# Products of 64 rows issued as side-by-side pairs in a three-block transformer kernel, the causal mask moved to VectorE, and GDN row sums padded to 128 rows

## The chip, the cores and the metric

The kernel runs on one core of a Trainium2 chip. The core has TensorE (matmul; the profile calls it PE, and its weight loads PEld), VectorE (DVE), ScalarE (ACT), GpSimd (POOL) and a queue engine (SP) that issues DMAs. Each engine works through its own list of instructions in the order in which the program has them, and waits for the others by semaphores. The metric is the device time of one execution in microseconds, the median of several; lower is better. About 0.2% of this kernel's time (6 us) is what a measurement can tell from no change.

## What is computed

Three blocks follow each other on 512 tokens of 1024 features: a block with a state-space scan (SSD) and a gated delta rule (GDN), a block with an RWKV scan and a sparse attention (DSA), and a block with a gated MLP and a differential attention. All arithmetic is float32. The parts that the change touches, cut to their core:

```
# GDN, per chunk of tokens: row sums of log decays, spread over all partitions
decay = exp(where(tril, gc[..., :, None] - gc[..., None, :], -inf))

# DSA, block 2: 8 heads of 64 features; index scores choose the keys, then softmax
sc        = einsum('bqhd,bsd->bqhs', iq, ik) * 64 ** -0.5
idx_score = einsum('bqhs,bqh->bqs', relu(sc), iw)          # top 256 keys are kept
p = softmax(einsum('bqhd,bqkhd->bqhk', q, k_sel) * 64 ** -0.5)
out = einsum('bqhk,bqkhd->bqhd', p, v_sel)

# RWKV, block 2: 8 heads of 64 features, one step per token (the kernel does it by chunks)
state = state * w_t + (state @ -kk_t) b_t^T + v_t k_t^T ;  y_t = state @ r_t

# differential attention, block 3: 8 heads, two 64-feature queries and keys each
p1 = softmax(causal(q1 @ k1.T / 8)) ; p2 = softmax(causal(q2 @ k2.T / 8))
o  = rms_norm((p1 - lam * p2) @ v)
```

## The kernel before

Features or tokens lie on the 128 partitions, 512 tokens or 128 features along the free dimension. Nearly all matmul work is linear layers: `mm3` (L216 to L218) and `lin_tm` (L245 to L247) split every float32 operand into two float32r parts and sum three products into a PSUM bank. Their weights come in by DMA, ScalarE makes the high part (L194) and VectorE the low part (L195).

PSUM has eight banks of 512 float32 columns. `ps_lin` gives two banks with the tag "pl" to the linear layers. `ps` gives two banks each with the tags "pa", "paa" and "pab": the plain stream and the streams "a" and "b", between which heads or chunks alternate. A name like `pa_20958` in a row is one such bank while it is in use.

The instructions are recorded in program order by the functions below; a scheduler then puts them in the fixed order in which each engine runs them. It fills TensorE's list between the steps of a scan or of an attention with products of linear layers that come before or after in the program, so the rows of an attention stand mixed with rows of L216 to L218.

A product "of 64 rows" contracts over 64 features and so occupies one half of the array's rows: features 0 to 63 of a tile or 64 to 127. A plain float32 product is two instructions in the trace. These are the 64-row products:

- `attend` of block 3 (L1736 and on; twice, once per half of the heads): for each of four blocks b of 128 queries, four heads and two maps m, the scores of 128 queries against (b + 1) * 128 keys. Keys ahead of the diagonal block are one product (L1751, absent for b = 0). In the diagonal block a bfloat16 product first puts the causal mask into PSUM (L1752), and the scores are summed onto it (L1753). VectorE takes the row maximum (L1754), ScalarE the exponential from PSUM (L1756); ScalarE and VectorE merge the two maps (L1760, L1761); TensorE transposes (L1764), ScalarE copies the transposes out (L1766), TensorE multiplies with v (L1769), ScalarE copies the result out (L1770). A norm of the whole block of queries follows.
- `attend` of block 2 (L1473 and on): for each b and each of eight heads, scores (L1480), mask and maximum in one VectorE instruction (L1483), exponential (L1486), transposes (L1489), copy (L1491), product with v (L1493). The streams "a" and "b" alternate by head; one bank of the plain stream collects the result of all eight heads.
- `rwkv_scan` (L1304): per chunk 16 products of 128 columns, four at a time for one row half, then four for the other, each four into one bank.
- `prepare` of the RWKV part (L1219, L1224) and `score` of the index scores (L1136).
- The GDN row sums (L712, L834) have 64 rows as well, because two parts of 32 columns are stacked.

`select` (L1152, L1153) picks the keys by 48 rounds of maximum and replacement on VectorE; it stands in VectorE's list next to the first half of the RWKV work.

## Time and profile before

| | |
|---|---|
| median of 3 runs | 3030.83 us (3030.61 to 3033.38) |
| the profiled execution: first to last instruction | 3028.6 us |
| PE busy | 2947.4 us, 97% |
| PEld busy | 2430.1 us, 80% |
| DVE busy | 1735.4 us, 57% |
| ACT busy | 1112.4 us, 37% |
| POOL busy | 46.9 us, 2% |
| mean granted clock of TensorE | 0.989 of full speed |

The profiled execution's span is 2.2 us under the median of the timed runs. A busy share is the union of an engine's instructions over the span. The end of a matmul is modelled and matmuls overlap, so start times say more about what a matmul costs than their durations do.

### The profile page before, as it was taken

What the parts mean: (1) busy time and instruction counts of PE and PEld (TensorE: products, weight loads), DVE (VectorE), ACT (ScalarE), POOL (GpSimd) and SP (SyncE); (2) the same over time, 40 slices, a digit from 0 to 9 for tenths busy, and PEclk for the clock granted to TensorE, in tenths of its full rate; (3) what the DMA queues carried; (4) which work ended last, traced back from release to release, by engine and by line L of the source; (5) the groups of instructions that cost most, each with busy time, mean ns of one, the idle gap of its engine ahead of it and who ended that gap; (6) DMA issues with size and microseconds to landing.
All of it is one profiled execution on the core that took longest, in us unless ns stands there. A gap on an engine that the chain in (4) does not pass through costs nothing. (4 is left out here: it accounts for less than half of the span.)

```text
span 3028.6 us, 39369 instructions
## 1 busy us (share of the span) xinstructions
PE 2947.4 (97%) x15170; PEld 2430.1 (80%) x15170; DVE 1735.4 (57%) x3871; ACT 1112.4 (37%) x2076; POOL 46.9 (2%) x95
## 2 busy tenths in 40 slices
PE   6999999999999999999999999999999999999999
PEld 4778888888788886788978878888987978888887
DVE  6787737655655457977653564333757563553343
ACT  4435424433322233333253332222465553332221
POOL 1000000000000000000000000000000000000000
PEclk9999999999999998999999999999999999999999
DMA  5222233233445322222113423333321214333332
GB/s 125 78 58 77 60 96 98 68 97 98 139 144 162 91 84 85 71 59 58 34 32 87 131 83 92 98 97 102 118 70 57 63 44 131 98 91 96 99 91 90
DMA packets 481660, 269.06 MB, mean 89 GB/s; under 512 B 30607, under 2 KB 469073, under 8 KB 481473
## 3 DMA queue, kind: packets, MB, share of 16 engines
q1 hardware_dynamic: 445680, 255.67, 28.9%
q10 hardware_dynamic: 33920, 9.44, 1.3%
q0 software_dynamic: 1872, 1.43, 0.6%
q8 instruction: 120, 1.97, 0.3%
q14 instruction: 68, 0.55, 0.1%
HBM read 252.20 MB, written 14.16 MB: 88 GB/s over the span
## 5 line engine op out<-in xcount | busy, mean ns | idle before, releaser
L194 ACT CAST wh<-wr 128x1024 fp32r<-128x1024 f32 (+3 forms) x447 | 454.0, 1016 | 1293.0 <-PE pl L217 914.3
L216 PE MATMUL pl<-h,wh 128*128 128x512 f32 x2224 | 878.8, 395 | 10.0 <-DVE long L1186 4.6
L218 PE MATMUL pl<-h,wl 128*128 128x512 f32 x2224 | 875.7, 394 | 11.5 <-DVE wl L195 11.5
L217 PE MATMUL pl<-h,wh 128*128 128x512 f32 x2224 | 878.0, 395 | 1.0 <-DVE h L195 1.0
L195 DVE TENSOR_TENSOR wl<-wr,wh 128x1024 fp32r<-128x1024 f32 (+3 forms) x447 | 525.9, 1177 | 413.3 <-ACT wh L194 402.0
L216 PEld LDWEIGHTS pl<-h,wh 128*128 128x128 f32 x2224 | 419.8, 189 | 100.6 <-DVE long L1186 5.4
L218 PEld LDWEIGHTS pl<-h,wl 128*128 128x128 f32 x2224 | 419.2, 189 | 100.9 <-DVE wl L195 14.8
L217 PEld LDWEIGHTS pl<-h,wh 128*128 128x128 f32 x2224 | 419.5, 189 | 90.3 <-issue 3.5
L217 PE MATMUL pl<-long,wh 128*128 128x512 f32 x648 | 252.9, 390 | 0.2 <-DVE long L195 0.2
L216 PE MATMUL pl<-long,wh 128*128 128x512 f32 x648 | 253.1, 391 | 0.0
L218 PE MATMUL pl<-long,wl 128*128 128x512 f32 x648 | 253.0, 390 | 0.0
L543 DVE SCALAR_TENSOR_TENSOR long<-pl,long 128x512 f32<-128x512 f32 x72 | 49.8, 691 | 178.3 <-PE pl L218 178.3
L216 PEld LDWEIGHTS pl<-long,wh 128*128 128x128 f32 x648 | 121.7, 188 | 26.3 <-issue 1.0
L218 PEld LDWEIGHTS pl<-long,wl 128*128 128x128 f32 x648 | 121.7, 188 | 25.6 <-issue 0.3
L217 PEld LDWEIGHTS pl<-long,wh 128*128 128x128 f32 x648 | 121.7, 188 | 25.4 <-DVE long L195 0.7
L531 DVE TENSOR_TENSOR tmp<-tmp,pl 128x512 f32<-128x512 f32 x66 | 45.3, 686 | 149.2 <-PE pl L218 149.2
L216 PE MATMUL pl<-tmpa,wh 128*128 128x512 f32 (+1 forms) x304 | 120.1, 397 | 3.4 <-ACT tmpa L322 3.4
L217 PE MATMUL pl<-tmpb,wh 128*128 128x512 f32 (+1 forms) x304 | 120.9, 398 | 0.1
L218 PE MATMUL pl<-tmpa,wl 128*128 128x512 f32 (+1 forms) x304 | 120.2, 396 | 0.0
L216 PEld LDWEIGHTS pl<-tmpa,wh 128*128 128x128 f32 (+1 forms) x304 | 57.3, 189 | 16.8 <-ACT tmpa L322 4.0
L217 PEld LDWEIGHTS pl<-tmpb,wh 128*128 128x128 f32 (+1 forms) x304 | 57.4, 189 | 13.2 <-DVE tmpb L323 1.3
L218 PEld LDWEIGHTS pl<-tmpa,wl 128*128 128x128 f32 (+1 forms) x304 | 57.5, 189 | 13.0 <-issue 0.7
(772 smaller groups left out, 4034.5 us busy)
## 6 DMA issues: line engine op xcount, KB each, us to landing
wr<-in_w_in SPq DMA_DIRECT2D x169, 512.0 KB, 3.7
wr<-in_w_ffn_in SPq DMA_DIRECT2D x44, 512.0 KB, 4.0
wr<-in_ffn_w_gate SPq DMA_DIRECT2D x44, 512.0 KB
wr<-in_ffn_w_up SPq DMA_DIRECT2D x44, 512.0 KB, 3.8
wr<-in_ffn_w_down SPq DMA_DIRECT2D x32, 448.0 KB, 3.7
wr<-in_w_ada SPq DMA_DIRECT2D x24, 512.0 KB, 3.5
wr<-in_w_out SPq DMA_DIRECT2D x16, 512.0 KB, 3.9
wr<-in_ffn_w_down SPq DMA_DIRECT2D x16, 512.0 KB, 3.9
```

The costliest lines, as they stand in the source:

```text
L194: self.nc.scalar.copy(hi, src)
L195: self.nc.vector.tensor_tensor(lo, src, hi.bitcast(F32), ALU.subtract)
L216: mm(ps, wh, xh, start=first, stop=False)
L217: mm(ps, wh, xl, start=False, stop=False)
L218: mm(ps, wl, xh, start=False, stop=last)
L531: nc.vector.tensor_tensor(t1, t1, ps, ALU.mult)
L543: nc.vector.scalar_tensor_tensor(x[i], ps, scale, x[i], ALU.mult, ALU.add)
```

## The change

The 64-row products of the two halves are issued directly after each other, into different banks. `side_by_side` records them and has the scheduler keep each next to the one before. In both attentions the two banks of a pair come from one double bank (`ps_pair`, tag "pq", two of them, four banks); for the time of an attention the pool of the tags "pa", "paa", "pab" is closed and opened anew (`banks`), and the transposes and results of all heads use the two plain banks "pa". In block 3 the mask products are gone: one VectorE instruction negates the scores, adds a tile `causal` (0, or 1e30 above the diagonal) and takes the minimum, and writes the result to SBUF, from which ScalarE takes the exponential. In block 2 the scores of two pairs of heads are asked for ahead of the four heads' own work. The RWKV products alternate between halves. The GDN row sums have 64 rows of zeros added (one memset on GpSimd). The linear layers' banks are a pool of their own.

```diff
+HALVES = slice(0, 64), slice(64, 128)
...
+    def side_by_side(self, calls):
+        mm = self.nc.tensor.matmul
+        mm(*calls[0], start=True, stop=True)
+        for c in calls[1:]:
+            with self.tc.high_priority():
+                self.tc.keep_in_program_order(mm(*c, start=True, stop=True))
+    def ps_pair(self):
+        t = self.pp.tile([P, 2 * S], F32, name=self.name("pq"), tag="pq", bufs=2)
+        return t[:, 0:S], t[:, S:2 * S]
...
-        rows = env.const([2 * n, S], FR, base=base + "rows")
+        rows = env.const([P, S], FR, base=base + "rows")
+        if 2 * n < P:
+            nc.gpsimd.memset(rows[2 * n:].bitcast(F32), 0.0)
...
-        return lambda col: (which[0:2 * n, col // 4:col // 4 + 1].to_broadcast([2 * n, P]), rows)
+        return lambda col: (which[:, col // 4:col // 4 + 1].to_broadcast([P, P]), rows)
...
             for right, mask in ((kt, mstr), (rt, minc)):
-                for e in range(2):
-                    ps = env.ps()
-                    rows = slice(e * 64, e * 64 + 64)
-                    for m, left in enumerate((bn, kd)):
-                        for j in range(2):
-                            mm(H(ps, 2 * m + j), left[j][rows, tok], right[j][rows, tok], start=True, stop=True)
+                two = [env.ps() for _ in range(2)]
+                env.side_by_side([(H(two[e], 2 * m + j), left[j][rows, tok], right[j][rows, tok])
+                                  for m, left in enumerate((bn, kd)) for j in range(2) for e, rows in enumerate(HALVES)])
+                for ps in two:
...
+        def scores(f):
+            out = env.ps_pair()
+            env.side_by_side([(ps[:, :n], qf[f][rows, b * P:(b + 1) * P], kf[f][rows, :n]) for ps, rows in zip(out, HALVES)])
+            return out
...
-        for hd in range(8):
-            with env.on("ab"[hd % 2]):
-                head(hd)
+        for q in range(2):
+            pairs = [scores(2 * q + j) for j in range(2)]
+            for j in range(2):
+                for e in range(2):
+                    with env.on("ab"[e]):
+                        head(4 * q + 2 * j + e, pairs[j][e])
...
-                if b:
-                    mm(ps[:, :n - P], qf[hd][rows, b * P:(b + 1) * P], kf[hd][rows, :n - P], start=True, stop=True)
-                mm(ps[:, n - P:n], env.identb, env.negmask_q, start=True, stop=False)
-                mm(ps[:, n - P:n], qf[hd][rows, b * P:(b + 1) * P], kf[hd][rows, n - P:n], start=False, stop=True)
-                nc.vector.reduce_max(st[:, 2 + m:3 + m], ps[:, :n], axis=mybir.AxisListType.X, negate=True)
+            two, ex = env.ps_pair(), []
+            env.side_by_side([(ps[:, :n], qf[hd][rows, b * P:(b + 1) * P], kf[hd][rows, :n]) for ps, rows in zip(two, HALVES)])
+            for m, ps in enumerate(two):
                 t = env.tmp()
-                nc.scalar.activation(t[:, :n], ps[:, :n], AF.Exp, bias=st[:, 2 + m:3 + m], accum_out=st[:, 4 + m:5 + m])
+                nc.vector.tensor_tensor_reduce(t[:, :n], ps[:, :n], causal[:, S - n:], -1.0, 3.0e38, ALU.add, ALU.min, st[:, m:m + 1])
+                nc.scalar.activation(t[:, :n], t[:, :n], AF.Exp, scale=-1.0, bias=st[:, m:m + 1], accum_out=st[:, 4 + m:5 + m])
...
-            ps = env.ps()
+            with env.on(""):
+                ps = env.ps()
...
-            po = env.ps()
+            with env.on(""):
+                po = env.ps()
```

Three places show what the scheduler made of it, all in TensorE's list.

**Block 3, second attention, 512 keys, before.** L1751 and L1753 are the scores, L1752 the mask with its weight load, L1764 transposes, L216 and L217 linear layers.

```order
L1751 MATMUL pa_20958<-long_20218,long_19832 128x384
L1752 LDWEIGHTS identb_73
L1752 MATMUL pa_20958<-negmaskq_92,identb_73 128x128
L1753 MATMUL pa_20958<-long_20218,long_19832 128x128
L1751 MATMUL pa_20965<-long_20218,long_19832 128x384
L1764 MATMUL pa_20944<-ident_72,tmpb_20931 128x128 x4
L1752 LDWEIGHTS identb_73
L1752 MATMUL pa_20965<-negmaskq_92,identb_73 128x128
L1753 MATMUL pa_20965<-long_20218,long_19832 128x128
```

The same place in the change, where L108 and L111 are the first product of a pair and the others, L1796 the transposes and L1802 the products with v.

```order
L1796 MATMUL pa_20732<-ident_75,tmpb_20722 128x128 x3
L237 MATMUL pl_21011<-long_19308,wh_21013 128x512
L108 MATMUL pq_20833<-long_20151,long_19765 128x512
L111 MATMUL pq_20833<-long_20151,long_19765 128x512
L1802 MATMUL pa_20738<-long_20270,tmpb_20736 128x128
L1802 MATMUL pa_20738<-long_20272,tmpb_20736 128x128
L1802 MATMUL pa_20738<-long_20274,tmpb_20736 128x128
L238 MATMUL pl_21011<-long_19309,wh_21013 128x512
```

Two score products, two mask products and two further score products of a head have become one pair; all transposes and results take "pa". From the first score product of this attention to its last product with v, 132 products of linear layers (512 columns) stood in the list before, and 94 stand there now; in the first attention of block 3 it was 96 and 96 of 256 columns, and is 89 and 46. What is taken out follows behind the attention.

**Block 2, attention, 512 keys, before.** L1480 is a head's score product, L1489 are transposes, L1493 products with v.

```order
L1489 MATMUL pa_13137<-ident_72,tmpb_13132 128x128 x4
L1480 MATMUL pa_13166<-long_12325,long_12086 128x512
L1493 MATMUL pa_13111<-long_12597,tmpb_13142 128x64
L1493 MATMUL pa_13111<-long_12599,tmpb_13142 128x64
L1493 MATMUL pa_13111<-long_12601,tmpb_13142 128x64
L1493 MATMUL pa_13111<-long_12603,tmpb_13142 128x64
```

The same in the change: L1516 are transposes, L1520 products with v.

```order
L1516 MATMUL pa_13133<-ident_75,tmpb_13128 128x128 x4
L239 MATMUL pl_13340<-long_12757,wl_13343 128x512
L237 MATMUL pl_13361<-h_9099,wh_13363 128x512
L238 MATMUL pl_13361<-h_9100,wh_13363 128x512
L239 MATMUL pl_13361<-h_9099,wl_13364 128x512
L1520 MATMUL pa_13105<-long_12599,tmpb_13138 128x64
L1520 MATMUL pa_13105<-long_12601,tmpb_13138 128x64
L1520 MATMUL pa_13105<-long_12603,tmpb_13138 128x64
L1520 MATMUL pa_13105<-long_12605,tmpb_13138 128x64
L108 MATMUL pq_13179<-long_12457,long_12204 128x512
L111 MATMUL pq_13179<-long_12457,long_12204 128x512
L1516 MATMUL pa_13149<-ident_75,tmpa_13144 128x128 x4
```

One plain bank holds the result of eight heads, so the transposes of all heads now go through the other one: between the transposes of a head and its products with v stand three or four products of a linear layer, or a pair of scores.

**RWKV scan, before.** L1304: four products of one half into one bank, then four of the other.

```order
L1304 MATMUL pa_1969_9873<-long_1895_9527,long_1926_9711 128x128
L1304 MATMUL pa_1969_9873<-long_1900_9561,long_1946_9786 128x128
L1304 MATMUL pa_1969_9873<-long_1895_9527,long_1905_9595 128x128
L1304 MATMUL pa_1969_9873<-long_1900_9561,long_1910_9629 128x128
L1304 MATMUL pa_1971_9881<-long_1895_9527,long_1926_9711 128x128
L1304 MATMUL pa_1971_9881<-long_1900_9561,long_1946_9786 128x128
```

In the change the banks, and with them the halves, alternate.

```order
L111 MATMUL pa_1970_9876<-long_1895_9529,long_1926_9713 128x128
L111 MATMUL pa_1969_9875<-long_1900_9563,long_1946_9788 128x128
L111 MATMUL pa_1970_9876<-long_1900_9563,long_1946_9788 128x128
L111 MATMUL pa_1969_9875<-long_1895_9529,long_1905_9597 128x128
L111 MATMUL pa_1970_9876<-long_1895_9529,long_1905_9597 128x128
L111 MATMUL pa_1969_9875<-long_1900_9563,long_1910_9631 128x128
```

Where all four products of a half had stood together, a product of one half is now followed by one of the other.

Outside these stages the list of TensorE is the same but for neighbours that changed places. Unbroken groups of 64-row instructions in it number 162 before and 72 now.

## Rows read from the trace of the kernel before

**Rows 1.** The page: the span, and busy time of each engine.

```profile
span 3028.6 us, 39369 instructions
PE 2947.4 (97%) x15170; PEld 2430.1 (80%) x15170; DVE 1735.4 (57%) x3871; ACT 1112.4 (37%) x2076; POOL 46.9 (2%) x95
```

**Rows 2.** Busy time of each engine in five stretches, with granted clock.

```profile
1170.00:1300.00 130.00, 119.84 (x546) 88.50 (x546) 119.88 (x310) 45.09 (x74) 4.31 (x8) 0.95 0.25 67
1300.00:1470.00 170.00, 167.53 (x1191) 146.86 (x1191) 126.06 (x461) 54.96 (x106) 12.24 (x24) 1.00 0.19 49
1522.00:1594.00 72.00, 72.00 (x376) 49.08 (x375) 35.43 (x140) 44.52 (x112) 0.00 (x0) 1.00 0.09 25
2227.00:2308.00 81.00, 80.76 (x457) 58.85 (x456) 47.54 (x152) 60.12 (x160) 0.00 (x0) 1.00 0.16 48
2411.00:2487.00 76.00, 75.96 (x404) 54.28 (x404) 47.73 (x157) 50.16 (x153) 0.00 (x0) 1.00 0.13 39
```

**Rows 3.** Timeline of PE in block 3's attention: start, duration, instruction.

```profile
2240.65 0.22 PE L1752 MATMUL pa<-negmaskq,identb 128*128 128x128 bf16 x1
2240.80 0.37 PE L1753 MATMUL pa<-long,long 64*128 64x128 f32 x1
2240.81 0.37 PE L1751 MATMUL pa<-long,long 64*128 64x128 f32 x1
...
2241.23 0.23 PE L1752 MATMUL pa<-negmaskq,identb 128*128 128x128 bf16 x1
2241.39 0.49 PE L1753 MATMUL pa<-long,long 64*128 64x128 f32 x2
2241.80 0.50 PE L217 MATMUL pl<-h,wh 128*128 128x512 f32 x1
...
2478.29 0.37 PE L1753 MATMUL pa<-long,long 64*128 64x128 f32 x1
```

**Rows 4.** Timeline in block 2's attention: PE and ACT.

```profile
1578.90 0.60 PE L1489 MATMUL pa<-ident,tmpb 128*128 128x128 f32 x4
...
1579.43 1.12 PE L1480 MATMUL pa<-long,long 64*128 64x512 f32 x2
1579.59 0.58 ACT L1491 COPY tmpb<-pa 128x512 f32<-128x512 f32 x1
...
1580.48 1.10 PE L1493 MATMUL pa<-long,tmpb 128*128 128x64 f32 x8
```

**Rows 5.** Timeline of PE in RWKV's `prepare`, in the stretch of `select`.

```profile
1282.02 0.69 PE L1219 MATMUL pa<-long,long 64*128 64x512 f32 x1
1282.03 0.69 PE L1224 MATMUL pa<-long,long 64*128 64x512 f32 x1
...
1287.76 0.80 PE L216 MATMUL pl<-h,wh 128*128 128x512 f32 x1 [4.61 <-DVE long L1186]
```

**Rows 6.** Timeline of PE in the RWKV scan.

```profile
1265.75 2.99 PE L1304 MATMUL pa<-long,long 64*128 64x128 f32 x30 [0.22 <-DVE tmpa L1307]
1268.67 0.50 PE L218 MATMUL pl<-h,wl 128*128 128x512 f32 x1
```

**Rows 7.** Timeline of PE: a linear product, row sums of SSD (128 rows), of GDN (64).

```profile
142.78 0.40 PE L218 MATMUL pl<-h,wl 128*128 128x512 f32 x1
143.02 0.39 PE L711 MATMUL pa<-negmask,identb 128*128 128x512 bf16 x1
143.06 0.58 PE L712 MATMUL pa<-ssdrows,which 128*128 128x512 f32 x1
...
245.08 0.38 PE L711 MATMUL pa<-negmask,identb 128*128 128x512 bf16 x1
245.39 0.49 PE L712 MATMUL pa<-gdnrows,which 64*128 64x512 f32 x1
```

**Rows 8.** ACT exponentials of 512 columns, from PSUM and from SBUF: count, busy us, mean ns.

```profile
L1756 ACT ACTIVATE tmpa<-pa,s 128x512 f32<-128x512 f32 x8 | 5.5, 688 | 4.5 <-DVE s L1754 4.5
L1486 ACT ACTIVATE tmpa<-tmpa,s,qs 128x512 f32<-128x512 f32 x4 | 3.3, 814 | 1.0 <-DVE s L1560 0.9
```

More of the change, by code (lines that the diff above doesn't have):

```diff
@@ L46, in __init__ @@
         self.sp = pool("small", bufs=1)
-        self.pp = pool("psum", bufs=1, space=PSUM)
+        self.lp = pool("linear", bufs=1, space=PSUM)
+        self.ctx, self.pp = ctx, None
+        self.banks()
         self.dp = pool("dram", bufs=1, space=bass.MemoryType.DRAM)
@@ L1133, in score @@
             for hd in range(8):
-                ps = env.ps()
-                rows = slice((hd % 2) * 64, (hd % 2) * 64 + 64)
-                mm(ps[:, :n], iqt[hd // 2][rows, b * P:(b + 1) * P], ikt[rows, :n], start=True, stop=True)
+                if hd % 4 == 0:
+                    four = []
+                    for j in range(2):
+                        for stream, rows in zip("ab", HALVES):
+                            with env.on(stream):
+                                four.append(env.ps())
+                            mm(four[-1][:, :n], iqt[hd // 2 + j][rows, b * P:(b + 1) * P], ikt[rows, :n], start=True, stop=True)
+                ps = four[hd % 4]
                 t = env.tmp()
@@ L1217, in prepare @@
             r, k, v = pa[i], pa[4 + i], pa[8 + i]
-            ps = env.ps()
-            mm(ps, ups[0:64, i * P:(i + 1) * P], wa[0:64, :], start=True, stop=True)
+            ps, ps2 = env.ps(), env.ps()
+            env.side_by_side([(out, ups[rows, i * P:(i + 1) * P], wa[rows, :]) for out, rows in zip((ps, ps2), HALVES)])
             lw = env.tmp()
@@ L1501, in attend @@
         otm.append(o)
+    env.banks()
     for b in range(NC4):
         attend(b)
+    env.banks()
     merged = [None] * 8
@@ L1766, in head @@
             nc.scalar.copy(pt[:, :n], ps[:, :n])
-            po = env.ps()
+            with env.on(""):
+                po = env.ps()
             for s in range(b + 1):
@@ L1802, in third_block @@
     qf, kf, vt = qk_half(Q0, 0, True), qk_half(K0, 1), v_half(0)
+    env.banks()
     o0 = attend(0, qf, kf, vt)
+    env.banks()
     wt, bs, ln = gmlp_consts()
@@ L1865, in third_block @@
     qf, kf, vt = qk_half(Q0 + S, 0), qk_half(K0 + S, 1), v_half(1)
+    env.banks()
     o1 = attend(1, qf, kf, vt)
+    env.banks()
     gated(GA0, a["a_w_proj_3"][0], ya, 4, True)
```

30 lines of the change are left out of this document (13 added, 17 removed).

## The prediction

> **What bounds the kernel.** I read the page first: TensorE is busy 2947.4 of 3028.6 us, no other engine over 57% [rows 1]. In a kernel whose TensorE is full nearly everywhere, what counts is the time in which TensorE could not start its next product. So I went to the stages that hold 64-row products and asked for the busy time by stretch [rows 2]. Four of the five stretches are full on PE (72.0 of 72, 80.8 of 81, 76.0 of 76, 167.5 of 170), with DVE and ACT at 32 to 74% of them. The exception is 1170 to 1300 us, where DVE is busy 119.9 of 130 us, as long as PE: `select` stands there, and PE's first product after 1282 us starts only at 1287.76, after a wait for DVE [rows 5]. The granted clock is 1.00 in the four, and 0.95 on average in the one with that wait.
>
> Then the timeline, from start to start. A lone 64-row product of 128 columns holds TensorE from 2241.39 to 2241.80, 0.41 us [rows 3]; one of 512 columns from 1579.43 to 1580.48, 1.05 us [rows 4]; so 0.21 us more for each further 128 columns, and 0.62 and 0.84 us between. Two products on opposite halves that stand next to each other already run together in the kernel before: L1753 and L1751 start at 2240.80 and 2240.81 and the next product starts at 2241.23, 0.43 us for both [rows 3]; two of 512 columns start at 1282.02 and 1282.03 [rows 5]. So the effect that the change asks for exists on this chip, and a pair costs what its longer member costs alone.
>
> **The change, part by part.** *Block 3's attention, 2227 to 2308 and 2411 to 2487 us.* Before, each of 16 score lists per block of queries (four heads, two maps, two attentions) has a mask product, 0.16 us from its start to that of the scores (2241.23 to 2241.39), then 0.41 us for the diagonal block, and for b = 1, 2, 3 another 0.41, 0.62, 0.84 us: 0.57 + 0.98 + 1.19 + 1.41 = 4.15 us, times 16 is 66.4 us. From that I take 20 places where L1753 and the next map's L1751 already run together (the first at 2240.80, the last at 2478.29 [rows 3]), 0.41 us each: 58 us. After: eight pairs per block of queries at 0.41, 0.62, 0.84, 1.05 us, 8 x 2.92 = 23.4 us. TensorE gets back **34.8 us**.
>
> *Block 2's attention.* 32 lone products, 8 x 2.92 = 23.4 us, become 16 pairs, 11.7 us. Each entry costs a little more: the last of four transposes starts about 1579.23 (0.60 us for four, 0.27 of it the last one's own length, by the same rows) and the scores 0.20 us later, where transposes follow each other at 0.11. 16 entries fewer at 0.09 us give 1.4: **13 us** together.
>
> *RWKV scan.* 30 instructions from 1265.75 to 1268.67 [rows 6] are 0.195 us per product of two; 128 products are 25 us. In pairs half: 12.5 us. About a quarter of the products, those of rows 6 among them, lies before 1300 us, where TensorE waits for VectorE anyway, and counts nothing: **9.5 us**.
>
> *GDN row sums.* With 128 rows, as in SSD, the sum follows its mask product after 0.04 us (143.02, 143.06); with 64 rows after 0.31 us (245.08, 245.39) [rows 7]. 14 sums (L712 eight, L834 six, the latter without a mask product, which I price alike) at 0.27 us: **3.8 us**. The memset on GpSimd is done long before its first reader; POOL is busy 46.9 us in all [rows 1].
>
> *`prepare` and `score`* stand in VectorE's stretch or between: **0**, bounded by 6 us (three pairs of 1.05 us saved, plus the quarter of the scan).
>
> Sum of TensorE time set free: 34.8 + 13 + 9.5 + 3.8 = 61 us. It counts only if TensorE has other work ready at that moment, and here I take off two terms.
>
> *ScalarE in block 3.* The exponential now reads what VectorE wrote to SBUF: 814 ns at 512 columns where it was 688 from PSUM [rows 8], 0.126 us on 32 exponentials, 4.0 us per attention. ScalarE was busy 50.2 of 76 and 60.1 of 81 us [rows 2]: 54 and 64 us after. TensorE's own work there falls to 76 - 17.4 - 38 x 0.24 = 49.5 us (38 linear products moved out, 0.24 us each, 142.78 to 143.02 [rows 7]) and 81 - 17.4 - 7 x 0.24 - 50 x 0.12 = 55.9 us (the ones of 256 columns at half). So ScalarE, which had slack, now holds more work in these two stretches than TensorE. Some of it leaves with the linear products, whose weights and results it handles. If enough leaves, the wait is nothing; if nothing leaves and ScalarE idles 10% of the time, it is 54/0.9 - 49.5 + 64/0.9 - 55.9 = 26 us. I take **13**. VectorE, at 47.7 and 47.5 us in the same rows, stays below both.
>
> The "TensorEngine Tiling (Array Packing)" page of the Trainium skill, section "PSUM Bottleneck", says the same in general: tiling makes TensorE faster and not the emptying of PSUM, and the copy out may become the limit. By the rows above the loss is 13 us and the sum 44; by that rule taken whole the stretches would keep their length, and the sum would be about 5, as worked out under the rivals. No row of before shows which.
>
> *The plain bank in block 2.* All heads' transposes now take one bank in turn. After the four transposes end (1579.50) the copy is done at 1580.17 [rows 4], 0.67 us later; the list puts three linear products (0.72 us) or a pair (1.05 us) there, so it is covered while ScalarE copies at once. Queued behind a products-with-v that waits are the next head's transposes and the linear products. ScalarE is busy 44.5 of 72 us there [rows 2], so a copy sometimes waits for part of an exponential of 0.81 us. I take **4 us** for 32 heads, between 0 and 10 (a 0.3 us delay each).
>
> 61 - 13 - 4 = 44 us. From the profiled 3028.6 us that is 2984.6; the median of the runs lies 2.2 us above the profiled span, so **2987 us**. Its own bounds: 61 + 6 = 67 gives 2964, 61 - 26 - 10 = 25 gives 3006.
>
> **The rivals.** *No new waits.* The scheduler has put enough linear products into both attentions, and all that is freed counts: 61 to 67 us, 2964 to 2970. For it: PE was full to 99% in these stretches before with the same kind of filling. Against: ScalarE's sum above.
>
> *ScalarE sets block 3's attentions.* The two stretches keep 76 and 81 us, though 17 us of linear products (9.1 + 7.7) have left them and are run later. Then 34.8 is not gained and 17 added: 61 - 34.8 - 17 - 4 = 5, 3026 us. Against: before, ScalarE was at most 74% busy and stood waiting for scores, so shorter scores must help it some.
>
> *Slower: the two plain banks.* Where three tags with six banks stood, transposes and results of all heads take turns in two: 32 heads x 2 in block 3 and 32 in block 2, 96 handovers, each of which ends only when ScalarE has copied. ScalarE works in order, so a copy can stand behind an exponential. If each handover costs TensorE over 61 / 96 = 0.64 us, the change loses; at a whole exponential of 0.81 us it is 78 us, and the time 3030.8 + 17 = 3048. Against: the copy in rows 4 starts 0.09 us after the last transpose ends, and other products stand in every handover of the list.
>
> *The pairs don't run together*, because one of the two waits for its bank. Then block 3 keeps 2 x 23.4 = 46.8 against 58 us, 11 gained, block 2 gains 1.4, GDN 3.8, the scan nothing; less 10 of waits that is 6, 3025 us. Against: in the list nearly all second products follow the first directly, and [rows 3, 5].
>
> **Chances.** My forecast, ScalarE eating a part, 0.60; no new waits 0.20; ScalarE sets block 3 0.08; the banks, slower, 0.06; pairs not together 0.06. The time is that of the first, 2987. The range holds the first two, from 2962 to 3012, with the upper end a little beyond 3006 toward the rivals at 3025. Faster by over 0.2% (6 us, about what a measurement can tell): the first two and half of the two near 3025, 0.87; within 0.2% 0.06; slower 0.07.
>
> **What would show it.** In the profile after: pairs L108 and L111 start within 0.02 us of each other, and the next product 0.42 to 1.05 us later. PE instructions of 64 rows are unchanged but for the merged ones and the mask is gone. Block 3's attentions are shorter than 76 and 81 us by 12 to 26 us each, with ACT over 85% busy and PE under 95%; PE's waits there name ScalarE's copies. Block 2's attention ends some 10 us sooner with short PE waits for L1518. GDN's sums start 0.04 us after their mask. 1170 to 1300 keeps its length. I am wrong if block 3's attentions keep their length (ScalarE or the banks), or if PE stays full there and the gain passes 60 us; or if a wait in one of these stages lets the granted clock fall to half.

## The result, and the profile after

The changed kernel takes **2985.09 us** (median of 4 runs, 2982.98 to 2987.55) against 3030.72 us before (4 runs beside it): ratio 0.9848, 95% interval 0.9836 to 0.986. The forecast was 2987.0, in a range of 2962 to 3012. The time is right; the terms behind it are not. The attentions brought 11 us more than forecast, the part with the RWKV scan brought 10 us less, and the two errors nearly cancel: that the sum came within 2 us is luck. (One correction to the cut of the reference above: with 512 tokens the sparse attention keeps 128 keys, not 256. Nothing in the argument uses the number.)

The page of the changed kernel: span, then busy time of each engine; its counterpart is [rows 1].

```profile
span 2985.5 us, 39119 instructions
PE 2892.7 (97%) x15010; PEld 2393.1 (80%) x15010; DVE 1727.3 (58%) x3936; ACT 1106.4 (37%) x2074; POOL 47.4 (2%) x96
```

The five stretches of [rows 2] as they lie now: length, busy time of PE, PEld, DVE, ACT and POOL, granted clock, DMA share, GB/s. The last three are block 2's attention and block 3's two, each from its first score product to the end of its last product with v.

```profile
1168.00:1300.00 132.00, 115.70 (x542) 87.69 (x542) 122.00 (x316) 43.49 (x73) 4.16 (x8) 0.93 0.26 68
1300.00:1468.00 168.00, 164.21 (x1195) 140.88 (x1194) 122.50 (x452) 55.66 (x107) 12.27 (x24) 0.99 0.20 51
1526.90:1590.70 63.80, 63.73 (x401) 47.06 (x401) 31.93 (x142) 46.53 (x113) 0.00 (x0) 1.00 0.11 30
2215.90:2275.00 59.10, 56.73 (x322) 39.16 (x322) 43.00 (x183) 53.04 (x150) 0.00 (x0) 1.00 0.18 54
2383.90:2437.30 53.40, 51.00 (x280) 34.49 (x280) 42.88 (x185) 44.63 (x144) 0.00 (x0) 1.00 0.14 40
```

The three attentions before, cut in the same way:

```profile
1522.90:1601.40 78.50, 78.50 (x413) 54.64 (x413) 36.29 (x146) 48.42 (x117) 0.00 (x0) 1.00 0.10 28
2227.90:2309.40 81.50, 81.26 (x462) 59.38 (x462) 48.28 (x153) 60.95 (x166) 0.00 (x0) 1.00 0.15 46
2412.00:2486.50 74.50, 74.46 (x394) 53.00 (x394) 47.24 (x156) 49.05 (x151) 0.00 (x0) 1.00 0.14 40
```

The three attentions are 15, 22 and 21 us shorter. In block 3's two TensorE is busy for 96% of the time and idle for 2.4 us each, where it was idle for 0.2 us and less; ScalarE is busy for 90% and 84%, and for 73% in block 2's. The first stretch has not become shorter, and its granted clock went from 0.95 to 0.93.

A stretch holds other linear products in the one kernel than in the other, so lengths alone do not give the gain. Both kernels run 11064 products of linear layers that the trace records. I numbered them by start time and compared the start of the same number in both traces; the difference between two numbers is what the work between them gained, in one profiled execution each (that of the changed kernel was the slowest of its four, 2987.55 us).

| work (numbers of the products) | forecast | measured |
|---|---|---|
| GDN (300 to 3900) | 3.8 | 1.9 |
| index scores, `prepare`, RWKV scan (3900 to 4650; before 1160.0 to 1513.5 us, after 1158.1 to 1511.8) | 9.5 | -0.2 |
| block 2's attention (4650 to 5200) | 13 - 4 = 9 | 13.5 |
| an FFN that nothing changed (5200 to 6000) | 0 | -1.6 |
| block 3's attentions (7000 to 8100, 8100 to 8850) | 34.8 - 13 = 21.8 | 15.3 + 13.0 = 28.3 |
| all | 44 | 42.0 |

The FFN's 1.6 us are the clock: between 1760 and 1820 us the granted clock is 0.5 for 13.7 us in after, for 10.2 us of that work before.

A pair of 512 keys in block 3's attention, PE's timeline after (start, duration, instruction):

```profile
2248.72 0.69 PE L108 MATMUL pq<-long,long 64*128 64x512 f32 x1
2248.72 0.69 PE L111 MATMUL pq<-long,long 64*128 64x512 f32 x1
2249.25 0.59 PE L108 MATMUL pq<-long,long 64*128 64x512 f32 x1
2249.26 0.59 PE L111 MATMUL pq<-long,long 64*128 64x512 f32 x1
2249.78 0.50 PE L237 MATMUL pl<-h,wh 128*128 128x512 f32 x1
```

The two halves start together, and the next product comes 1.06 us after the first: the forecast's 1.05.

PE's waits from 1155 to 1515 us, after (line that waited, what for: us in all, times, longest):

```profile
PE pa L485 <- DMA tmpa<-blocks: 10.0, 1, 10.0
PE pl L237 <- DVE long L1214: 3.1, 3, 2.5
PE pa L1266 <- ACT long L1258: 2.6, 1, 2.6
```

L485 transposes the diagonal blocks that `tri_inv` inverts by substitution for the first scan. Before, its two waits in this stretch sum to 2.6 us, and the wait that stood there was the 4.61 us of [rows 5]. VectorE's timeline in the first half of the 10.0 us, after:

```profile
1281.35 0.99 DVE L476 TENSOR_TENSOR tmpa<-tmpa 32x512 f32<-32x512 f32 x1
...
1282.36 0.68 DVE L1180 MAX8 s<-long 128x8 f32<-128x512 f32 x1
1282.96 0.66 DVE L477 TENSOR_REDUCE s<-tmpa 32x64 f32<-32x512 f32 x1
1283.55 0.15 DVE L472 TENSOR_TENSOR tmpb<-tmpb 32x12 f32<-32x12 f32 x1
...
1283.70 0.66 DVE L1181 MATCH_REPLACE8 long<-s,long 128x512 f32<-128x512 f32 x1
1284.29 1.05 DVE L478 TENSOR_TENSOR tmpa<-tmpa,s 32x512 f32<-32x512 f32 x1
...
1285.35 0.67 DVE L1180 MAX8 s<-long 128x8 f32<-128x512 f32 x1
1285.96 0.66 DVE L479 TENSOR_REDUCE tmpa<-tmpa 32x64 f32<-32x512 f32 x1
```

Between each two steps of the substitution (L472 to L479) for one chunk stand steps for the other chunk and a round of `select` (L1180, L1181). What TensorE waits for goes at the pace of this list until the last step (L479) ends at 1286.62 us; the blocks then go to DRAM and back by two DMAs, and TensorE starts 4.8 us later, at 1291.43. The clock around that wait, after, in stretches (columns as above), and last the clock behind the 4.61 us wait of [rows 5], before:

```profile
1230.00:1281.00 51.00, 50.37 (x282) 40.39 (x280) 47.10 (x137) 15.83 (x25) 4.16 (x8) 1.00 0.25 65
1281.00:1291.40 10.40, 0.44 (x4) 0.00 (x1) 10.40 (x21) 0.42 (x1) 0.00 (x0) 0.67 0.12 28
1291.40:1301.40 10.00, 9.56 (x33) 7.73 (x34) 8.57 (x17) 2.06 (x4) 0.00 (x0) 0.50 0.52 134
```

```profile
1287.70:1301.30 13.60, 10.26 (x38) 8.53 (x39) 10.85 (x20) 2.54 (x5) 0.00 (x0) 0.50 0.34 89
```

While TensorE waits the granted clock falls to 0.50 (1.2 of 2.4 GHz) and stays there for 10 us more of work. The same happened before: behind the shorter wait the clock stood at 0.50 for 13.6 us, with TensorE busy for 10.3 of them. So the half clock at this place is not new; the longer wait is.

How the part from 3900 to 4650 spends its time, before and after:

```profile
1160.00:1513.50 353.50, 340.48 (x2140) 283.76 (x2139) 273.32 (x861) 116.74 (x212) 16.55 (x32) 0.98 0.22 58
1158.10:1511.80 353.70, 333.56 (x2140) 277.13 (x2139) 272.35 (x860) 115.53 (x211) 16.43 (x32) 0.97 0.23 60
```

TensorE is idle for 13.0 us before and 20.1 after, and works at half clock for 10.3 us before and 16.6 after. If work at half clock counts half, TensorE's own work has fallen from 335.3 to 325.2 us. So the pairs of this part did free 10 us of TensorE; 7.1 of them came back as idle time and 3.1 as half clock. (The ends of matmuls are modelled, so this split is an estimate.)

### The profile page after: what moved, and what is told of

Read it like the earlier page. It is cut to its first block, busy times and chain, and to the rows that moved or that the text cites. A ratio compares the mean times of both kernels' runs of the same rounds, so it can differ in the third digit from the quotient of the medians.

```text
span 2985.5 us, 39119 instructions
## 1 busy us (share of the span) xinstructions
PE 2892.7 (97%) x15010; PEld 2393.1 (80%) x15010; DVE 1727.3 (58%) x3936; ACT 1106.4 (37%) x2074; POOL 47.4 (2%) x96
## 5 line engine op out<-in xcount | busy, mean ns | idle before, releaser
L239 PE MATMUL pl<-h,wl 128*128 128x512 f32 x2224 | 877.2, 395 | 12.9 <-DVE wl L216 12.9
L237 PE MATMUL pl<-h,wh 128*128 128x512 f32 x2224 | 880.5, 396 | 8.5 <-DVE long L1214 3.1
L216 DVE TENSOR_TENSOR wl<-wr,wh 128x1024 fp32r<-128x1024 f32 (+3 forms) x447 | 526.1, 1177 | 432.0 <-ACT wh L215 424.3
L239 PEld LDWEIGHTS pl<-h,wl 128*128 128x128 f32 x2224 | 419.9, 189 | 103.6 <-DVE wl L216 16.4
L237 PEld LDWEIGHTS pl<-h,wh 128*128 128x128 f32 x2224 | 420.2, 189 | 99.7 <-DVE long L1214 5.3
L239 PE MATMUL pl<-long,wl 128*128 128x512 f32 x648 | 253.1, 391 | 0.0
L237 PE MATMUL pl<-long,wh 128*128 128x512 f32 x648 | 252.9, 391 | 0.0
L239 PEld LDWEIGHTS pl<-long,wl 128*128 128x128 f32 x648 | 121.7, 188 | 25.5 <-issue 0.8
L237 PEld LDWEIGHTS pl<-long,wh 128*128 128x128 f32 x648 | 121.7, 188 | 24.7
L237 PE MATMUL pl<-tmpa,wh 128*128 128x512 f32 (+1 forms) x304 | 120.9, 399 | 3.6 <-ACT tmpa L343 3.6
L239 PE MATMUL pl<-tmpa,wl 128*128 128x512 f32 (+1 forms) x304 | 120.4, 396 | 0.0
L237 PEld LDWEIGHTS pl<-tmpa,wh 128*128 128x128 f32 (+1 forms) x304 | 57.4, 189 | 16.9 <-ACT tmpa L343 4.4
L238 PEld LDWEIGHTS pl<-tmpb,wh 128*128 128x128 f32 (+1 forms) x304 | 57.6, 190 | 13.3 <-DVE tmpb L344 1.1
L239 PEld LDWEIGHTS pl<-tmpa,wl 128*128 128x128 f32 (+1 forms) x304 | 57.5, 189 | 13.0 <-issue 0.5
```

Of the source, the lines that this page charges most:

```text
L216: self.nc.vector.tensor_tensor(lo, src, hi.bitcast(F32), ALU.subtract)
L237: mm(ps, wh, xh, start=first, stop=False)
L238: mm(ps, wh, xl, start=False, stop=False)
L239: mm(ps, wl, xh, start=False, stop=last)
```

## The experiments

**Theory:** from 1158 to 1512 us VectorE's list, with `select` in it, sets the pace, and what the pairs freed there turned into the wait for the substitution; in the attentions TensorE's time is all that counts, ScalarE takes next to nothing. **Rivals:** the scan's pairs are worth their 9.5 us and something else cost as much; or ScalarE and the banks did cost the 17 us taken off, and the attentions freed more than thought.

All times are medians; the kernel before took 3029 to 3031 us beside them. "RWKV" is the time from linear product 3900 to 4650, "half clock" the time with a granted clock of 0.5 in that part, "busy in it" how much of that TensorE worked, "idle" how long TensorE stood still in the part, all from the one profiled execution.

| kernel | us | ratio to before, 95% | RWKV | half clock | busy in it | idle |
|---|---|---|---|---|---|---|
| before | 3030.72 | | 353.5 | 13.7 | 10.3 | 13.0 |
| changed | 2985.09 | 0.9836 to 0.986 | 353.6 | 23.9 | 16.6 | 20.1 |
| scan as before | 2991.30 | 0.9854 to 0.9881 | 356.3 | 23.9 | 19.1 | 15.8 |
| index scores, `prepare` as before | 2986.99 | 0.9832 to 0.9862 | 357.7 | 30.7 | 23.9 | 17.2 |
| no rounds | 2963.72 | 0.9762 to 0.9789 | 334.6 | 0 | 0 | 8.4 |
| no rounds, scan as before | 2967.12 | 0.9783 to 0.9809 | 337.6 | 0 | 0 | 6.8 |
| rounds after the first scan | 3025.15 | 0.9974 to 0.9992 | 390.2 | 64.9 | 23.1 | 56.6 |
| late rounds | 2991.85 | 0.9853 to 0.9882 | 358.1 | 34.1 | 25.5 | 20.4 |
| rounds after both scans | 2982.74 | 0.9832 to 0.9862 | 342.4 | 10.2 | 9.5 | 11.2 |
| the same, scan as before | 2991.88 | 0.9865 to 0.9897 | 352.7 | 20.5 | 20.5 | 10.9 |
| rounds after the last substitution | 2980.39 | 0.9826 to 0.9853 | 339.0 | 6.8 | 6.7 | 11.9 |
| mask only | 3014.97 | 0.993 to 0.9955 | | | | |
| copies on VectorE | 2986.24 | 0.9835 to 0.9869 | | | | |
| more on ScalarE | 3003.40 | 0.9899 to 0.9929 | | | | |

### The scan's pairs, with and without the rounds of `select`

```diff
-                two = [env.ps() for _ in range(2)]
-                env.side_by_side([...])
-                for ps in two:
+                for e in range(2):
+                    ps = env.ps()
+                    rows = slice(e * 64, e * 64 + 64)
+                    for m, left in enumerate((bn, kd)):
+                        for j in range(2):
+                            mm(H(ps, 2 * m + j), left[j][rows, tok], right[j][rows, tok], start=True, stop=True)
```

> The changed kernel, but the RWKV scan's 128 products stand as before: four for one row half, then four for the other. Theory: from 1158 to 1512 us VectorE's list (select and the substitution of tri_inv) and the DMAs behind it set the time, and what the pairs freed turned into the 10.0 us wait of the transposes L485. Then the pairs of the scan are worth nothing here: 2985 us, within 3 us of the changed kernel, and that wait is shorter by about what the scan takes longer. Rival: the pairs are worth the 9.5 us of the forecast and something else in the change costs as much there: 2993 to 2997 us.

The RWKV part takes 2.7 us longer than in the changed kernel, and L485 waits 2.7 us in two pieces, the longest 2.0, instead of 10.0. But the waiting has in part only another name: ahead of L485 stands a linear product (L237) that waits 4.4 us for VectorE, with the half clock behind it as ever. TensorE's own work is 5.8 us more than with the pairs (half clock counted half), its idle time 4.3 less. So the theory holds in kind, since most of what the scan's pairs free comes back as waiting, and not to the full. The medians leave it open how much the pairs are worth: they differ by 6.2 us, between theory and rival, with intervals that overlap. This profiled execution was the fastest of its four (2985.80 us at a mean granted clock of 0.989; the others 2991 to 2993 at 0.986 and 0.987), and the changed kernel's was its slowest, so the traces show the pairs' worth too small rather than too large.

```diff
-            for _ in range(16):
+            for _ in range(0):
...
-            nc.vector.tensor_scalar(acc[:, :n], acc[:, :n], -2.9e38, -1.0e30, op0=ALU.is_gt, op1=ALU.mult)
+            nc.vector.tensor_scalar(acc[:, :n], acc[:, :n], -2.9e38, 0.0, op0=ALU.is_gt, op1=ALU.mult)
```

> The changed kernel without the 48 rounds of maximum and replacement in select; the masks of the sparse attention are then 0 but for the causal corner, so this leaves out part of the computation. Theory: VectorE loses 48 x 1.4 = 67 us of work from 1178 to 1300 us; the waits that stand behind it (10.0 us at L485, 3.1 at L237, 2.6 at L1266) and the half clock after the long one go: 12 to 30 us less than the changed kernel, 2955 to 2973 us. Rival: the waits come from DMAs and from the order of TensorE's own list: within 4 us of 2985.

> As the kernel without the rounds of select, and the scan's products as before (four for one half, then four for the other). Theory: with VectorE free TensorE sets this stage, and now the scan's pairs count: 7 to 12 us slower than the kernel without the rounds and with pairs (TensorE's time on these products was 29.5 us before and is about 22 after). Rival: the pairs save nothing in the scan at all, because each product is too short: within 2 us of it.

PE's waits from 1155 to 1515 us without the rounds, with the scan's pairs:

```profile
PE pa L485 <- DMA tmpa<-blocks: 2.7, 2, 1.8
PE pl L237 <- DVE long L1214: 1.8, 2, 1.3
PE pa L1266 <- ACT long L1258: 1.3, 1, 1.3
```

Without the rounds (56 us of VectorE's work by the trace, not 67) the part is 19 us shorter, no wait passes 2 us and the clock does not fall in it: VectorE's rounds cost 19 us here, as the theory had it, 11.7 of idle time and some 8 of half clock (16.6 us of work at half speed). But its second half missed. With VectorE free the scan's pairs are worth 3.0 us by the trace and 3.4 by the medians, not 7 to 12. TensorE's own time, from each start to the next, says where the rest is. On the 64-row products of scan and `prepare` it is 27.7 us with the scan's pairs and 35.0 without, so 7.3 less; on the linear products it is 6.4 more (179.6 against 173.2), in many small pieces, and on the others 2.1 less. In all, its own work is 4.6 us less and its idle time 1.6 more. So the theory holds for the wait and not for the pairs' worth: with VectorE free, over half of the 7.3 us still came back in the products around them.

### `prepare` and the index scores

```diff
-                if hd % 4 == 0:
-                    four = []
...
-                ps = four[hd % 4]
+                ps = env.ps()
+                rows = slice((hd % 2) * 64, (hd % 2) * 64 + 64)
+                mm(ps[:, :n], iqt[hd // 2][rows, b * P:(b + 1) * P], ikt[rows, :n], start=True, stop=True)
...
-            ps, ps2 = env.ps(), env.ps()
-            env.side_by_side([(out, ups[rows, i * P:(i + 1) * P], wa[rows, :]) for out, rows in zip((ps, ps2), HALVES)])
+            ps = env.ps()
+            mm(ps, ups[0:64, i * P:(i + 1) * P], wa[0:64, :], start=True, stop=True)
...
+            ps = env.ps()
+            mm(ps, ups[64:128, i * P:(i + 1) * P], wa[64:128, :], start=True, stop=True)
```

> The changed kernel with the products of the index scores and of prepare as before, one at a time; the scan keeps its pairs. Theory: in this stretch these pairs are worth nothing or less, because what they save comes back as the wait for the substitution and as half clock behind it: 2981 to 2987 us. Rival: TensorE's time on the index scores fell from 16.5 to 12.6 us, and that counts: 2988 to 2991 us.

2986.99 us, no difference that can be told; the RWKV part has 357.7 us and much the same wait of 9.9 us at L485. TensorE's own work is 3.3 us more without these pairs, and it works 7.3 us longer at half clock. What the pairs are worth is within the few microseconds that the half clock moves.

### Where the rounds stand

```diff
-            for _ in range(16):
-                nc.vector.max(out=m8, in_=acc[:, :n])
+            for k in range(16):
+                top = nc.vector.max(out=m8, in_=acc[:, :n])
+                if b == 1 and k == 0:
+                    env.tc.keep_in_program_order(top)
...
     scan(0)
+    select()
     rkv_lin(1)
-    select()
```

> The changed kernel with the same work, but select's first round is held in VectorE's list behind the first RWKV scan, so that its rounds no longer stand between the steps of that scan's substitution. Theory: the 10.0 us wait and the half clock behind it go, TensorE's freed time counts: 2970 to 2978 us. Rival: VectorE's sum of work sets the stage, wherever the rounds stand, and the wait moves into the second scan: 2982 us or more.

The theory's number fell and the rival's held: 3025.15 us. The list now has 32 rounds in a row, with nothing between them, and the low part of a weight tile (L216) stands behind them: TensorE waits 24.4 us for it at L239, and 13.5 us at L1452 for another result of VectorE. The rounds do not cost by their place in the first scan alone.

```diff
+    def rounds(b, pin=False):
...
+        for _ in range(16):
+            top = nc.vector.max(out=m8, in_=acc[:, :n])
+            if pin:
+                env.tc.keep_in_program_order(top)
...
+            yield
...
     def select():
-        for b in range(1, NC4):
+        for b in (1, 2):
+            for _ in rounds(b):
+                pass
+        late.append(rounds(3, True))
...
+    def some(k):
+        for _ in range(k):
+            next(late[0], None)
...
     def q_epi(i, ps):
...
+        some(2)
...
     def k_epi(i, ps):
...
+        some(2)
...
     k_lin()
+    some(20)
```

> The changed kernel with the same work; the 16 rounds of select for the last block of queries, which stood between the steps of the first scan's substitution, are put two at a time behind the results of the q and k products, later in VectorE's list. Theory (where the rounds stand is what counts, the 19 us that the kernel without rounds gained are VectorE's): the 10.0 us wait before L485 goes, no wait as long comes in its place, 5 to 14 us less: 2971 to 2980 us. Rival (as with all rounds behind the scan: later rounds hold up the weights' low parts and the second scan): 2985 us or more.

The rival again, with 2991.85 us: the 10.0 us wait is gone and one of 8.5 us at L485 stands in the second scan, between whose substitution steps the rounds now are.

```diff
     scan(1)
+    some(1)
     q_lin()
```

> As the kernel with late rounds, but the first of select's 16 last rounds is held in VectorE's list behind the second scan, so that these rounds stand in neither scan's substitution and most of them between the maxima of block 2's attention. Theory (a wait arises wherever rounds stand between the substitution's steps; in the first case in the first scan, with late rounds in the second): both waits of 8 to 10 us are gone, and the time is 6 to 14 us under the changed kernel's, 2971 to 2979 us. Rival: block 2's attention, with 22 us more on VectorE (31 of 56 us before that), then waits for the maxima: 2985 us or more.

> The same placing of the rounds, and the scan's products as before, four for one row half and then four for the other. Theory (the scan's pairs save TensorE 7 us, some 4 of them come back at products that start alone, and the rest counts once no long wait for the substitution follows): 2 to 5 us slower than the one with pairs. Rival 1 (the forecast): 9 us slower. Rival 2 (the pairs are worth nothing in the scan at all): within 1 us.

With neither scan holding late rounds the RWKV part falls by 11.2 us to 342.4. Block 2's attention, between whose maxima the rounds now stand, gains only 5.7 us over before instead of 13.5, and the time is 2982.74 us, between the theory's range and the rival's: 2.4 of the 11 us arrive. Here the scan's pairs are worth 9.1 us by the medians and 10.2 us in the RWKV part, the forecast's size. Half of that is the clock: without pairs TensorE works 11.0 us longer at a granted 0.50, which costs 5.5 us; its own work is 5.1 us more. The largest piece at half clock has no wait at its start. Without the scan's pairs, the stretches around it:

```profile
1340.00:1350.20 10.20, 10.20 (x89) 9.77 (x87) 3.93 (x10) 3.36 (x8) 0.00 (x0) 1.00 0.08 21
1350.30:1360.40 10.10, 10.10 (x50) 10.00 (x48) 5.01 (x21) 2.13 (x5) 1.68 (x4) 0.50 0.00 0
```

PE is busy throughout. Ahead of the fall stand mostly small products, 14 of two columns each among them, 0.11 us apiece from 1347.58 to 1349.12:

```profile
1347.58 0.34 PE L1279 MATMUL pa<-bones,tmp 128*128 128x2 f32 x2
1347.78 0.36 PE L1279 MATMUL pa<-bones,long 128*128 128x2 f32 x2
...
1349.43 1.05 PE L1362 MATMUL pa<-tmpa,tmpa 128*128 128x64 f32 x8
```

That these small products bring the clock down would be a guess from their place, and the sister run speaks against it: with the scan's pairs the same 14 products stand at 1350.6 to 1351.9 us, and the clock stays at 1.00 from 1330 to 1370. What brings it down here stays open.

```diff
             z = env.tri_inv([h4(mats[0])[:, 0:2, :], h4(mats[1])[:, 0:2, :]])
+            if b == 1 and c == 3:
+                some(1)
...
     scan(1)
-    some(1)
     q_lin()
```

> The changed kernel with select's 16 last rounds held in VectorE's list behind the last substitution of the second scan only, so that most of them stand between the end of that scan and the first maxima of block 2's attention. Theory: the stretch up to the attention keeps the 11 us that the kernel with the rounds behind the whole second scan gained there, and the attention gives back less of them than the 8 us that it lost with the rounds between its maxima: 2972 to 2979 us. Rival (VectorE's sum of work up to the attention's end counts, wherever the rounds stand): 2981 to 2986 us.

The best time of the study that leaves no work out, 2980.39 us, with an interval that overlaps the changed kernel's; it lies between the theory's range and the rival's, half a microsecond from the rival's. The RWKV part is at 339.0 us, 14.6 less than in the changed kernel; block 2's attention gives back 11.8 of it (it gains 1.8 over before, not 13.5). PE's longest wait there, and in the second fence the 10.2 us at half clock that begin before the attention:

```profile
PE pq L108 <- DVE s L1527: 5.3, 1, 5.3
```

```profile
1517.70:1527.90 10.20, 5.48 (x19) 3.87 (x19) 10.20 (x35) 3.39 (x11) 0.00 (x0) 0.50 0.19 51
```

VectorE is busy for all of the 10.2 us. So the stall goes where the rounds go: leaving them out gains 21 us by the medians, and no place that was tried for them gains more than 5, nor clearly any. That VectorE's sum of work up to the end of block 2's attention is the limit fits these runs; a better place is not ruled out.

### ScalarE and the attentions

> The kernel before, with the causal mask of block 3's attention on VectorE and the exponential read from SBUF, and each map's scores one product; nothing is paired and the banks stay as they were. In the list the two maps of a head mostly stand apart in the first attention and next to each other about half of the time in the second. Theory (TensorE's time is all that counts there, ScalarE takes nothing): the products take 23 us instead of 28 in the first and 16 to 18 instead of 27 in the second attention, so 13 to 17 us less than before: 3013 to 3018 us. Rival 1 (most of block 3's 28 us come from the mask and the entries that it cost, not from the pairs): 3003 to 3008 us. Rival 2 (the forecast's deduction: exponentials from SBUF make ScalarE the bound): 3024 us or more.

```diff
-                if b:
-                    mm(ps[:, :n - P], ...)
-                mm(ps[:, n - P:n], env.identb, env.negmask_q, start=True, stop=False)
-                mm(ps[:, n - P:n], ..., start=False, stop=True)
-                nc.vector.reduce_max(st[:, 2 + m:3 + m], ps[:, :n], axis=mybir.AxisListType.X, negate=True)
+                mm(ps[:, :n], qf[hd][rows, b * P:(b + 1) * P], kf[hd][rows, :n], start=True, stop=True)
...
-                nc.scalar.activation(t[:, :n], ps[:, :n], AF.Exp, ...)
+                nc.vector.tensor_tensor_reduce(t[:, :n], ps[:, :n], causal[:, S - n:], -1.0, 3.0e38, ALU.add, ALU.min, st[:, m:m + 1])
+                nc.scalar.activation(t[:, :n], t[:, :n], AF.Exp, scale=-1.0, ...)
```

3014.97 us, 16 less than before; by the numbered products 6.2 + 7.6 = 13.8 us. TensorE's time on scores and masks, from each start to the next, is 56.1 us before (the forecast had 58), 38.2 with the mask moved, 23.8 in the changed kernel: 18 freed and 13.8 arrived for the mask, 14.4 freed and 14.5 arrived for the pairs. Rival 2 is out, since with the exponentials read from SBUF TensorE is nearly as busy as before (74.8 of 75.3 us in the first attention, 68.9 of 70.3 in the second); so is rival 1.

> The changed kernel with the copies of the transposed weights (block 2's and block 3's attentions, 64 copies) on VectorE instead of ScalarE, so ScalarE has about 10 us less work in each of block 3's attentions. Theory: ScalarE did not set the end of these stretches (TensorE is 97% busy there), so there is at most the 3 us of waits in each to win: 2979 to 2986 us. Rival (the 13 and 4 us that the forecast took off were truly lost to ScalarE, and TensorE's gain was larger than forecast): 2968 to 2975 us.

```diff
-            nc.scalar.copy(pt[:, :n], ps[:, :n])
+            nc.vector.tensor_copy(pt[:, :n], ps[:, :n])
```

2986.24 us, the same; the three attentions gain 1.4 us by the numbered products. (The copies are 6.7 us of ScalarE's work in each of block 3's attentions by the trace, not 10.) ScalarE's work was not what set their end.

> The changed kernel with 32 more ScalarE copies in each of block 3's attentions, each tile of scores onto itself ahead of its exponential: about 0.56 us each, 18 us in each attention, so that ScalarE, busy 58.6 of 68 and 50.1 of 69 us, would hold 76 and 68 us. Theory (ScalarE is felt only where its work passes TensorE's in the stretch): 8 to 20 us slower than the changed kernel, 2993 to 3005 us, and TensorE's waits in these stretches name ScalarE. Rival (linear products fill every wait that ScalarE makes): 2990 us or less.

```diff
+                nc.scalar.copy(t[:, :n], t[:, :n])
                 nc.scalar.activation(t[:, :n], t[:, :n], AF.Exp, scale=-1.0, ...)
```

3003.40 us, 18 slower, for 36 us of added work. Block 3's attentions with the added copies, the first 59 and 58 us of each, then the waits of the first that name ScalarE:

```profile
2211.00:2270.00 59.00, 51.97 (x253) 32.26 (x251) 37.90 (x163) 55.96 (x167) 0.00 (x0) 0.94 0.14 41
2392.00:2450.00 58.00, 53.35 (x278) 34.21 (x276) 42.84 (x184) 54.37 (x176) 0.00 (x0) 1.00 0.13 37
```

```profile
PE pa L1803 <- ACT tmpa L1799: 2.2, 1, 2.2
PE pa L1803 <- ACT tmpb L1799: 1.0, 2, 0.6
```

Now ScalarE is 95% and 94% busy and TensorE 88% and 92%: this is how a stretch looks that ScalarE sets. About half of TensorE's waits in the first name ScalarE, the other half VectorE; and at a granted clock of 0.94 some 3 of the 18 us are the clock's. Over each whole attention ScalarE is busy for 92% and 90% here, against 90% and 84% in the changed kernel, where 6.7 us less on ScalarE in each won 1.0 us in both together. So the share alone does not tell the two cases apart. "TensorEngine Tiling (Array Packing)" of the Trainium skill, section "PSUM Bottleneck", says that after a fourfold speed-up by tiling the copy out of PSUM may become the limit; for the twofold tiling of the changed kernel the trace shows no such limit (TensorE idle for 2.4 of 59.1 and of 53.4 us). The kernel with more work on ScalarE is no test of that sentence, since its added copies read and write SBUF.

## Why the prediction came out as it did

**Block 3's attentions (34.8 - 13).** The pairs and the mask freed 32 us by TensorE's starts (56.1 down to 23.8), and 28.3 arrived. The failed step is that ScalarE "now holds more work in these two stretches than TensorE", and the 13 taken for it. TensorE's sums came out as forecast: 56.7 and 51.0 us busy, against 55.9 and 49.5. ScalarE's did not: 53.0 and 44.6 us, against 64 and 54. Two things were wrong in them. The 0.126 us more for an exponential from SBUF compared two kinds of exponential: the 814 ns of [rows 8] are block 2's, which take their scale from a tile; block 3's, with a constant scale, went from 688 to 720 ns, and all 32 of an attention from 16.8 to 17.8 us, 1 us more and not 4:

```profile
L1787 ACT ACTIVATE tmpa<-tmpa,s 128x512 f32<-128x512 f32 x4 | 2.9, 720 | 0.0
```

And what leaves with the linear products was not subtracted, although the forecast names it: in the first attention three casts of weights (7 before, 4 after, 1.0 us each) and the reading of linear results by L1818 of before (3.7 us with its table load, none after). With that, TensorE's sum was the larger one, and the measured loss is 4 us, the time that TensorE stood idle. Of the signs, "shorter than 76 and 81 us by 12 to 26 us each" came true, "ACT over 85%" in one of the two (90% and 84%), and "PE under 95%" just missed (96%); the waits name VectorE more often than ScalarE's copies.

**Block 2's attention (13 - 4).** 13.5 us measured, and it ends 10.7 us sooner, as the forecast's sign had it. TensorE's scores went from 23.5 to 11.9 us and the transposes from 11.1 to 8.2, the products with v from 17.3 to 18.5: 13.3 us where the forecast had 13. The step "I take 4 us" for the plain bank was wrong: TensorE is busy for 63.7 of its 63.8 us, and the copies on VectorE gained 0.3 us there.

**RWKV scan (9.5).** Two things failed. "In pairs half": 30 instructions take from 1267.68 to 1269.66 us, 1.98 us, where they took 2.92 [rows 6]. That is a third less, not half, so 128 products give 8 us rather than 12.5. The starts say why: before, 8 of the 29 steps between these instructions are already under 0.07 us, where the halves change, and most others 0.11; after, every other one is 0.01 and the rest 0.11. The 0.2 us at the start and at the end of such a group stay:

```profile
1267.68 1.04 PE L111 MATMUL pa<-long,long 64*128 64x128 f32 x13
1268.46 0.27 PE L108 MATMUL pa<-long,long 64*128 64x128 f32 x1
1268.57 0.27 PE L111 MATMUL pa<-long,long 64*128 64x128 f32 x1
1268.57 0.27 PE L108 MATMUL pa<-long,long 64*128 64x128 f32 x1
1268.68 1.05 PE L111 MATMUL pa<-long,long 64*128 64x128 f32 x14
1269.66 0.50 PE L238 MATMUL pl<-h,wh 128*128 128x512 f32 x1
```

And the step by which only the quarter before 1300 us counts nothing: of the 10 us that all pairs of this part freed, 7.1 came back as TensorE's idle time and 3.1 as half clock. The scan's own pairs take 4.6 to 5.8 us off TensorE's work in each of the three comparisons. What of it shows is 2.7 us in the changed kernel, 3.0 without the rounds, and 10 with the rounds moved, where half of the 10 is the clock. That a wait "lets the granted clock fall to half" stood in the forecast as a way to be wrong; it happened here, but it had happened before as well, at the same place behind the 4.61 us wait, which the 0.95 of [rows 2] hides in its average.

**`prepare` and `score` (0).** Right as a price, and "1170 to 1300 keeps its length" holds (product 4280, near 1300 us, starts 1.2 us earlier than before, and the work ahead of product 3900 had already brought 1.9), with VectorE busy for 122.0 of 132 us.

**GDN (3.8).** 1.9 us. The sums after a mask start 0.03 us behind it, as forecast (0.31 before), 8 times. The six without a mask, "which I price alike", had no such gap: they start 0.15 us behind their neighbour before and after. What they gain is at their other end, where the next linear product starts 0.33 us behind them and not 0.42. So 8 x 0.28 + 6 x 0.09 = 2.8 us was all there was; the eleven other kernels with the same sums gain 0.0 to 2.8 us between the same two products.

```profile
243.90 0.38 PE L734 MATMUL pa<-negmask,identb 128*128 128x512 bf16 x1
243.93 0.58 PE L735 MATMUL pa<-gdnrows,which 128*128 128x512 f32 x1
```

**The rivals.** Slower by the banks: 96 handovers cost no more than the 4 us lost in block 3, far from 0.64 us each, if all of it were theirs. Pairs apart: all ran together. ScalarE sets block 3: shown only with 18 us added to each attention. "No new waits" was nearly right for the attentions, where TensorE came to stand idle for 4.8 us in block 3, and wrong for the RWKV part, where TensorE's idle time grew by 7.1 us, most of it in the wait of 10.0 us.

**Open.** Why the granted clock fell in one order of the RWKV part and not in another, where no long wait stands ahead; how much of the 15 us by which RWKV fell with the rounds behind the last substitution a better place could keep; and why the linear products around the scan take longer when its products are paired.

## What to carry to other kernels

A stretch that is 98% busy on the engine you relieve can still give nothing, if a chain through another engine ends just before it: freed time is paid out at the next wait, so price it at the end of the whole dependent part. Where a scheduler fills gaps with independent products, the other engines' work on these products leaves with them: take it off both sums before you set one engine's work in a stretch against another's. A price for an instruction is that of its own form; an exponential with its scale from a tile is no price for one with a constant scale. Cut a stretch before and after at the same work, not at like lengths. A half-array pair costs what its longer member costs alone, so long products gain half; short ones in groups, which already overlapped where the halves changed, gained a third here.

## What was not expected of the hardware

The granted clock followed the order of the work: 0 us at 0.50 in the RWKV part without the rounds, 23.9 us with them, 64.9 us with the worst order. In the changed kernel it fell during a wait of 10.0 us and stayed at 0.50 for 10 us of full work behind it; in the kernel before it stood at 0.50 for 13.6 us behind a wait of 4.61 us. In the kernel with the rounds after both scans and the scan as before it fell as well at 1350.3 us, where TensorE had been busy without a gap. An exponential of 512 columns took 720 ns from SBUF and 688 from PSUM with a constant scale, and 814 from SBUF with its scale from a tile.
